# Layer 0 of a two-layer attention trunk: attention steps ordered by a planner, with half of the output projection placed among them

## The chip, the core and the metric

The kernel runs on one core of one Trainium2 chip. The metric is the device time of one execution in microseconds; the kernel before was timed at 2638.1 us (median of three runs, 2637.88 to 2638.44).

## What is computed

A decoder trunk on 1024 positions of width 1024, in float32, two layers. Layer 0 mixes with sparse attention of three branches, layer 1 with forgetting attention; both add four heads of attention into 256 memory tokens, project all heads with one output matrix, add the residual, and end with a gated feed-forward block. Only layer 0's attention and its output projection are touched:

```python
def block(args):                        # layer 0, 12 heads in 2 groups
    s = einsum(qc, kc) * scale          # 64 compressed blocks
    p_cmp = masked_softmax(s, cmp_end[None, :] <= t[:, None])
    ...                                 # with 16 blocks of 64 and top 16: all causal keys
    s = einsum(qc, kg) * scale
    p = masked_softmax(s, m_sel)
    ...                                 # keys of the last 512 positions
    s = einsum(qc, kw) * scale
    p = masked_softmax(s, m_win)
    return g[..., 0:1] * o_cmp + g[..., 1:2] * o_slc + g[..., 2:3] * o_win
...
o_mem = memory_attention(q_mem, mem, mem_norm[l], w_mem_kv[l])
x = x + concatenate([o_mix, o_mem], axis=-1) @ w_o[l]
x = x + conv_ffn(rms_norm(x, ffn_norm[l]), w_up[l], conv_w[l], conv_b[l], w_down[l])
```

## The kernel before

Every float32 operand of a matmul is split into an upper part (rounded to the matmul's input type, written by ScalarE, line 81) and a lower part (the rest, written by VectorE, line 82); `mm3` (lines 156 to 158) makes one product from three matmuls of up to 512 columns.

The work of layer 0 follows in this order: `layer0_proj` (norm, keys, values, compressed keys, the queries of heads 0 to 3), `layer0_attn` (attention), `out_proj` (output projection, residual, norm), then the feed-forward block.

Attention is cut into units: one head and one half `c` of the queries (`c` = 0 is the first 512 positions). There are 24 units of the three-branch attention and 8 units of memory attention. For a unit, the scores of a row tile go to a two-bank PSUM tile `psa` (line 301, two such tiles exist); VectorE takes the row maximum (line 318), ScalarE the exponent with its sum into SBUF (lines 334 and 337); VectorE inverts the sum (lines 346 and 347) and GpSimd scales by that and the gate (line 358). Then TensorE transposes 128x128 pieces into PSUM `psb` (line 391; four such banks), four to a step; ScalarE writes their upper part `pt` (line 398), VectorE the lower part (line 401), and TensorE multiplies both with the values (line 414) into the unit's output in another `psb`. A finished unit is copied to `ob` (line 504) and stored to DRAM (line 506); when both heads of a pair of rows are there, `operand` loads them again (line 471), adds the two halves on GpSimd (line 472) and splits them into `oT`.

The exponents of each of the four kinds (selected or window branch, `c` 0 or 1) have a buffer of their own (tags `ps0`, `ps1`, `pw0`, `pw1`, one each; memory units `pm`, two). The order is written by `attention`: at every step `k` it emits the maxima and exponents of the scores begun one step ago, the transposes of step `k`, new scores as `pace` has due, one slice of the projection of later queries while such work lasts (`work`, `rope_proj`, `plain_proj`), and the value products of step `k - 2`. Tile's scheduler then fixes each engine's order.

The units run head by head, `c` = 0 and 1 in turn. `out_proj` comes behind the last unit: for each half `n` of the columns and each of 8 row tiles, 24 matmuls of 512 columns into a `psb` bank, an addition to the residual `x` (line 862), and in the second half the norm of the finished row tile (`norm_part`), its transposes (line 894) and splits. All DMAs are issued by SyncE in one queue, in order.

## Time and profile before

| what | value |
| --- | --- |
| median of three runs | 2638.1 us |
| profiled execution, its own time | 2643.0 us |
| its span | 2640.9 us |
| TensorE busy | 2506.7 us, 95% |
| VectorE, ScalarE, GpSimd busy | 71%, 50%, 28% |
| layer 0's attention, first score to last value product | 192 to 673 us |
| layer 0's output projection | 672 to 765 us |

How to read it: the span is what the profiler saw between the first and last instruction. Matmuls overlap in the pipeline, so the duration of one (some 0.39 us at 512 columns) is longer than the distance from its start to the next one's start when nothing is waited for, and TensorE can count as busy while it is slowed by a late operand. For TensorE the count of matmuls in a stretch, times that distance, tells more than its busy share.

### The profile page before, as it was taken

To read this page: it belongs to the slowest core of one execution; us is meant where nothing else is said; L and a number is where in the kernel's file an instruction comes from. 1 tells how busy PE (TensorE), PEld (TensorE's weight loads), DVE (VectorE), ACT (ScalarE), POOL (GpSimd) and SP (SyncE) were. 2 spreads that over 40 slices of the span, in tenths; PEclk is the share of its full clock that TensorE was granted. 3 is DMA by queue.
4 is the path that set the end of the run, shared out by engine and by line. 5 is a ranking of instruction groups with operands and counts; after the bars stand their busy time and mean duration, and the time that the engine had idled before them with its cause. 6 is when DMAs were issued, how large, how long until landed. Compare 5 with 4: busy or idle time off the path is not lost.

```text
span 2640.9 us, 36023 instructions
## 1 busy us (share of the span) xinstructions
PE 2506.7 (95%) x12642; PEld 2073.0 (78%) x12642; DVE 1881.6 (71%) x2822; ACT 1331.5 (50%) x2553; POOL 751.2 (28%) x616
## 2 busy tenths in 40 slices
PE   7899899988999999998999999999999999998998
PEld 6787777776877888886888988887777888886886
DVE  5757677878377787877765467778576877787765
ACT  4437576768245454544454356656334545443443
POOL 0105344445133545543000000000223555454000
PEclk9999999999999999999999999999999999999999
DMA  8473123334422323337434556656532333337523
GB/s 243 142 206 109 53 81 100 89 108 136 153 88 82 102 96 109 108 125 273 133 128 128 160 171 194 188 177 181 197 112 69 104 112 100 101 105 262 186 90 118
DMA packets 302702, 357.72 MB, mean 135 GB/s; under 512 B 37961, under 2 KB 183225, under 8 KB 302521
## 3 DMA queue, kind: packets, MB, share of 16 engines
q1 hardware_dynamic: 302520, 355.41, 42.8%
q8 instruction: 100, 1.64, 0.3%
q14 instruction: 82, 0.66, 0.1%
HBM read 245.55 MB, written 109.78 MB: 135 GB/s over the span
## 4 chain that ended last, share of the span: by engine, by line
PE 71%; DVE 9%; DMA 6%; ACT 6%; POOL 4%; issue 3%; SPq 1%; POOLq 0%; ACTq 0%; DVEq 0%
PE psa L156 11%; PE psa L157 11%; PE psa L158 11%; PE psb L156 8%; PE psb L158 8%; PE psb L157 8%; PE psa L301 5%; PE psb L414 4%; PE psb L391 3%; DVE pt L401 2%; DVE stat L318 2%; POOL gs L1350 1%; DMA hT<-in_w_down_dram 1%; ACT ps L334 1%; POOL pw L358 1%
## 5 line engine op out<-in xcount | busy, mean ns | idle before, releaser
L81 ACT ACTIVATE wh<-wr 128x512 fp32r<-128x512 f32 (+2 forms) x254 | 193.1, 765 | 353.9 <-PE psb L158 147.2
L82 DVE TENSOR_TENSOR wl<-wr,wh 128x512 fp32r<-128x512 f32 (+2 forms) x254 | 241.6, 955 | 165.5 <-ACT wh L81 164.8
L1335 DVE SCALAR_TENSOR_TENSOR v<-u,cw,v 128x1023 f32<-128x1023 f32 (+1 forms) x176 | 273.1, 1552 | 68.7 <-ACT v L1333 65.8
L401 DVE TENSOR_TENSOR pt<-psb,pt 128x512 fp32r<-128x512 f32 (+2 forms) x380 | 245.7, 657 | 87.2 <-ACT pt L398 84.6
L398 ACT ACTIVATE pt<-psb 128x512 fp32r<-128x512 f32 (+2 forms) x380 | 217.5, 583 | 130.9 <-PE psb L391 129.5
L1333 ACT ACTIVATE v<-u,cw 128x1024 f32<-128x1024 f32 x88 | 109.6, 1245 | 310.2 <-DVE u L1322 283.4
L414 PE MATMUL psb<-pt,vv 128*128 128x512 f32 (+2 forms) x864 | 232.2, 366 | 12.4 <-DVE pt L401 9.0
L156 PE MATMUL psa<-hT,wh 128*128 128x512 f32 x560 | 219.2, 392 | 5.3 <-DVE u L1296 5.3
L301 PE MATMUL psa<-kk,qq 128*128 128x512 f32 (+4 forms) x792 | 196.4, 359 | 25.0 <-ACT ps L334 14.7
L158 PE MATMUL psa<-hT,wl 128*128 128x512 f32 x560 | 218.6, 390 | 0.8 <-DVE wl L82 0.8
L157 PE MATMUL psa<-hT,wh 128*128 128x512 f32 x560 | 218.5, 390 | 0.0
L318 DVE TENSOR_REDUCE stat<-psa 128x1 f32<-128x640 f32 (+7 forms) x288 | 200.6, 714 | 21.5 <-PE psa L301 20.3
L334 ACT ACTIVATE ps<-psa,stat 128x128 f32<-128x128 f32 (+2 forms) x224 | 156.7, 706 | 59.6 <-DVE stat L318 53.7
L120 POOL TENSOR_TENSOR rs<-ss,consts 128x1 f32<-128x1 f32 x44 | 25.8, 588 | 516.3 <-DVE ss L118 378.0
L472 POOL TENSOR_TENSOR wr<-wr 128x512 f32<-128x512 f32 x32 | 42.3, 1323 | 440.7 <-DMA wr<-o 426.6
L414 PEld LDWEIGHTS psb<-pt,vv 128*128 128x128 f32 x864 | 141.4, 195 | 30.8 <-DVE pt L401 16.1
L301 PEld LDWEIGHTS psa<-kk,qq 128*128 128x128 f32 x792 | 125.8, 194 | 47.3 <-ACT ps L334 23.6
L156 PE MATMUL psb<-hT,wh 128*128 128x512 f32 x384 | 160.0, 417 | 2.2 <-DVE rt L607 1.8
L156 PE MATMUL psb<-wh 128*128 128x512 f32 x352 | 139.3, 396 | 20.7 <-ACT wh L81 20.6
L1237 POOL TENSOR_TENSOR ws<-wr 128x512 f32<-128x512 f32 x44 | 74.7, 1699 | 295.6 <-DMA wr<-in_w_up_dram 213.2
L391 PE MATMUL psb<-consts,ps 128*128 128x128 f32 x928 | 150.7, 280 | 8.1 <-DVE pt L401 4.9
L158 PE MATMUL psb<-hT,wl 128*128 128x512 f32 x384 | 151.7, 395 | 0.0
(285 smaller groups left out, 6853.1 us busy)
## 6 DMA issues: line engine op xcount, KB each, us to landing
wr<-in_w_up_dram SPq DMA_DIRECT2D x88, 512.0 KB
wr<-gd SPq DMA_DIRECT2D x154, 256.0 KB
gd<-v SPq DMA_DIRECT2D x88, 256.0 KB
gd<-gs SPq DMA_DIRECT2D x66, 256.0 KB
o<-ob SPq DMA_DIRECT2D x128, 128.0 KB
wr<-o SPq DMA_DIRECT2D x32, 512.0 KB
hT<-in_w_down_dram SPq DMA_DIRECT2D x64, 256.0 KB
qd<-st SPq DMA_DIRECT2D x56, 256.0 KB
```

Of the source, the lines that this page charges most:

```text
L81: nc.scalar.activation(hi, src, AF.Copy)
L82: nc.vector.tensor_tensor(lo, src, f32(hi), ALU.subtract)
L156: mm(out, lh, rh, start=first, stop=False, skip_group_check=more)
L157: mm(out, lh, rl, start=False, stop=False, skip_group_check=more)
L158: mm(out, ll, rh, start=False, stop=last, skip_group_check=more)
L301: nc.tensor.matmul(out, w, rhs, start=b not in banks[:i], stop=b not in banks[i + 1:])
L318: nc.vector.reduce_max(br["stat"][:, 0, ii:ii + 1], s[:, o:o + w], axis=AX.X, negate=True)
L391: nc.tensor.transpose(tp[0:kb, x:x + P], br["pt"][ii][:, o:o + kb], self.ident)
L398: nc.scalar.activation(st["hi"], st["src"], AF.Copy)
L401: self.nc.vector.tensor_tensor(st["lo"], st["src"], f32(st["hi"]), ALU.subtract)
L414: self.nc.tensor.matmul(out, v, t, start=st["begin"] and i == 0, stop=st["end"] and i == len(mms) - 1)
L1335: nc.vector.scalar_tensor_tensor(v[:, d:], u[:, :S - d], cw[:, tap, i:i + 1], v[:, d:], ALU.mult, ALU.add)
```

## The change

A class `Plan` is added. Every piece of layer 0's attention stage becomes a task with an engine, a duration written into the code, the tasks that it waits for, a priority and the buffers that it takes and gives back. `Plan.run` plays the tasks through such engines, each engine starting the ready task with the lowest priority number, and the tasks are then emitted in the order of their starts; Tile keeps that order on TensorE, ScalarE, VectorE and GpSimd (`manual_schedule`). SyncE's DMAs are still ordered by Tile.

Besides the order: the two value products of a step (from the upper and from the lower part) are tasks of their own. The four exponent tags and `pm` become one tag `p` of three buffers. The units are reordered: heads 0 to 5 as before with the first-half memory units among them, then for heads 6 to 11 the `c` = 0 units run ahead of the `c` = 1 units (`a` and `b` in the code). The output projection of the first 512 positions (`out_tasks`, 8 tiles of 24 matmuls) is cut into pieces of 6 matmuls that stand among the attention steps; its result with the residual goes to DRAM (`xr`). `out_half` then does the other 512 positions; it loads `w_o`'s first column half a second time, and normalises row tiles 0 to 3, read back from `xr`, in its first half. The lower parts of weights and rotated queries and keys are written by GpSimd in place of VectorE; the factor `QSC` moves into the rotation's tables; the gates are laid out so that the copy and product per unit (lines 826 and 828) fall away.

```diff
+    def run(self):
...
+            for e in engines:
+                skipped, q = [], ready[e]
+                while q and not busy[e]:
+                    x = heapq.heappop(q)
+                    t = self.tasks[x[1]]
+                    if not self.can(t):
+                        skipped.append(x)
+                        continue
+                    self.take(t["acq"], 1)
+                    order.append(t)
...
+                    heapq.heappush(events, (now + t["us"], 1, t["id"]))
...
+            t["fn"]()
+
...
-    def split(self, src, hi, lo, scale=None):
+    def split(self, src, hi, lo, scale=None, low=None):
...
             nc.scalar.activation(hi, src, AF.Copy)
-            nc.vector.tensor_tensor(lo, src, f32(hi), ALU.subtract)
...
+    def planned(self, ap, pool, l, od, units, works, lead, src):
...
+        steps, users, done, last = [], {}, {}, ([], [])
...
+        start = pl.add("SP", 15.0, lambda: None)
...
+                tag, _, bufs = br["p"]
+                same = users.setdefault(tag, [])
+                br["before"] = same[-bufs] if len(same) >= bufs else None
+                same.append(br)
+            deps = [(done[n, u["at"][1]], 6.0) for n in u["needs"]] + [start]
+            deps += [s_last[k - 2] if k > 1 else None, w_last[k - 3] if k > 2 else None, *(n_last[k - 4] if k > 3 else ())]
+            deps += [x for i in u.get("takes", ()) for x in (s_last[i], w_last[i])]
...
+                           [t_prev] + [ready[id(x[0]), ii] for x in st["ps"] for ii in x[2]], q, ["tp"])
+                hi = pl.add("ACT", 0.18 + 0.82e-3 * n, lambda st=st: self.upper_p(ap, st), [t], q, ["pt"])
+                lo = pl.add("DVE", 0.15 + 1.04e-3 * n, lambda st=st: self.lower_p(st), [hi], q, (), ["tp"])
+                us, o = sum(self.columns(len(x[2]) * P) for x in st["ps"]), ["o"] if st["begin"] else ()
+                if st["ps"][0][0]["kb"] == P:
+                    v = pl.add("PE", us, lambda st=st: self.value(st, 0), [hi, v_prev], q + 1.5, o)
+                    v_prev = pl.add("PE", us, lambda st=st: self.value(st, 1), [lo, v], q + 1.6, (), ["pt"])
+                else:
+                    v_prev = pl.add("PE", us, lambda st=st: self.value(st, 0), [lo, v_prev], q + 1.6, o, ["pt"])
...
+        k0, k1 = max(k for (c, _), ts in outs.items() if c == 0 for _, k in ts) + 6, len(steps) + 2
+        xr, w_o = self.dp.tile([CH, D], F32, name=f"xr{l}"), {}
+        before = [None, None]
+        for n in range(2):
+            prio = [k0 + (k1 - k0) * (16 * n + i) / 32 for i in range(16)]
+            ws = [self.w_o_tasks(pl, l, w_o, k, n, [split, before[-1]], prio[0] - 4) for k in range(0, KT, 2)]
+            for t in range(4):
+                before.append(self.out_tasks(pl, pool, oT[0], w_o, n, t, ws, [parts[0, kt] for kt in range(KT)], before[-2:], prio[4 * t:4 * t + 4],
+                                             src, xr))
...
+    def out_tasks(self, pl, pool, o, w_o, n, t, ws, parts, before, prio, src, xr):
...
+        def mms(i):
+            if i == 0:
+                x["ps"] = self.psb()
+            for k in range(2):
+                kt = 2 * i + k
+                wh, wl = w_o[n, i]
+                self.mm3(x["ps"], [p[:, kt, t * P:(t + 1) * P] for p in o["t"]], (wh[:, k, :], wl[:, k, :]), kt == 0, kt == KT - 1)
+
+        def add():
+            nc.vector.tensor_tensor(x["x"], x["ps"], x["x"], ALU.add)
+            nc.sync.dma_start(xr[t * P:(t + 1) * P, cs], x["x"])
+        ld, pe = pl.add("SP", 0.0, load, [ws[0], before[0]], prio[0]), before[1]
+        for i in range(4):
+            pe = pl.add("PE", 1.37, lambda i=i: mms(i), [pe, ws[i], parts[2 * i], parts[2 * i + 1]], prio[i], ["pb"] if i == 0 else (),
+                        ["wh"] if t == 3 else ())
+            pl.fill.append(pe)
+        return pl.add("DVE", 0.7, add, [pe, (ld, 4.0)], prio[3], (), ["pb"])
...
+                        def lo(half=half, s_=s_):
+                            st = x["st", half]
+                            nc.gpsimd.tensor_tensor(st[:, 1, :], x["r", half], f32(st[:, 0, :]), ALU.subtract)
...
         w = self.a["a_w_in"][0]
         self.n_pt, self.n_q = 3, 2
         with self.tc.tile_pool(name="l0a", bufs=1) as ap:
-            def mem_q(m):
...
+            def mem_q(m, *at):
+                return self.plain_tasks(("m", m), at, cpool, h, w, 1572 + m * P, self.qm0, m, QSC)
+            works = [self.rope_tasks(("q", 1), ((-3, 30), (30, 58)), cpool, h, w, 256, self.qd0, P), mem_q(0, (58, 68), (140, 150)), mem_q(1, (68, 80), (150, 160)),
+                     self.rope_tasks(("q", 2), ((80, 115), (118, 140)), cpool, h, w, 512, self.qd0, 2 * P)]
...
-            mem = list(self.mem_units(ap, self.qm0, self.mem[0], [("pm", 1024, 2)] * 2, lambda h: ("m", h // 2), "pool"))
-            units = nsa[:12] + mem[0:2] + nsa[12:16] + mem[2:4] + nsa[16:20] + mem[4:6] + nsa[20:22] + mem[6:8] + nsa[22:]
-            return self.attention(ap, 0, od, units, work, 6, 9)
...
+
+            a, b, c, d = nsa[12::2], nsa[13::2], mem[0::2], mem[1::2]
+            units = nsa[:8] + c[0:1] + nsa[8:10] + c[1:2] + nsa[10:12] + c[2:4]
+            g1 = len(units)
+            units += a[0:2] + b[0:1] + a[2:4] + b[1:2] + a[4:6] + b[2:3] + d[0:1] + b[3:4] + d[1:2] + b[4:5] + d[2:4] + b[5:6]
...
+            self.n_ob = 1
+            return self.planned(ap, cpool, 0, od, units, works, 5, self.a["x"][0])
...
-        t_s, t_w, t_c = [("ps0", 1280, 1), ("ps1", 3328, 1)], [("pw0", 1280, 1), ("pw1", 2560, 1)], ("pc", 256, 2)
+        t_s, t_w, t_c = [("p", 3328, 3)] * 2, [("p", 3328, 3)] * 2, ("pc", 256, 2)
...
-                        gt = self.sb(ap, [P, 3, 4], F32, "gt", 2)
-                        nc.vector.tensor_copy(gt, self.gates[:, c * 4:(c + 1) * 4, h * 3:(h + 1) * 3].rearrange("p t b -> p b t"))
-                        if c == 0:
-                            nc.vector.tensor_tensor(gt[:, 0, 0:1], gt[:, 0, 0:1], self.rv, ALU.mult)
+                        gt = self.gates[:, c, h * 3:(h + 1) * 3, :]
...
+    def out_half(self, l, oT, pool, fx, up, src):
...
+        self.residual(pool, src, xr, (0, 4, 1, 5, 2, 6, 3, 7))
+        for n in (1, 0):
+            if n == 0:
+                w = self.load_block(a["w_o"][l], [(0, CH)])
+                up.load(0)
...
+                ps, o = two[:, t % 2 * CH:(t % 2 + 1) * CH], (t - 4) * P
+                for i, kt in enumerate((0, 1, 2, 6, 7, 3, 4, 5)):
+                    self.mm3(ps, (oT[1][0][:, kt, o:o + P], oT[1][1][:, kt, o:o + P]), w(kt, 0, CH), i == 0, i == KT - 1)
+                xs = self.x[:, t, n * CH:(n + 1) * CH]
+                nc.vector.tensor_tensor(xs, ps, xs, ALU.add)
...
+                for f in turns:
+                    f()
...
-    def residual(self, pool, src):
+    def residual(self, pool, src, first, order):
         self.x = pool.tile([P, NT, D], F32, name=self.nm("x"))
-        for t in range(NT):
-            self.nc.sync.dma_start(self.x[:, t, :], src[t * P:(t + 1) * P, :])
+        for t in order:
```

TensorE at the head of the attention stage. The first rows are of the kernel before: `psb_1913` is a projection tile of later queries (heads 4 to 7), `psa_1685` and `psa_1736` the first unit's scores.

```order
L157 MATMUL psb_1913<-hT_93,wh_1697 128x512
L158 MATMUL psb_1913<-hT_92,wl_1698 128x512
L301 MATMUL psa_1685<-kk_261_1657,qq_265_1672 128x128
L301 MATMUL psa_1736<-kk_261_1657,qq_265_1672 128x512
L301 MATMUL psa_1685<-kk_261_1657,qq_266_1673 128x128
```

The same place in the changed kernel: `psb_1710` and `psb_1798` are such projection tiles, `psa_1773` and `psa_1787` the first unit's scores.

```order
L246 MATMUL psb_1710<-hT_91,wh_1672 128x512
L247 MATMUL psb_1710<-hT_90,wl_1673 128x512
L390 MATMUL psa_1773<-kk_273_1729,qq_277_1744 128x128
L390 MATMUL psa_1773<-kk_273_1729,qq_278_1745 128x128
...
L390 MATMUL psa_1787<-kk_273_1729,qq_278_1745 128x512
L390 LDWEIGHTS identb
L390 MATMUL psa_1787<-caub,identb 128x128
L245 MATMUL psb_1798<-hT_92,wh_1669 128x512
L246 MATMUL psb_1798<-hT_93,wh_1669 128x512
```

Before, 96 projection matmuls of later queries (four tiles of 24) stand ahead of the first score; now 48 do, and the other 48 come behind it.

TensorE near the end of the attention stage. Before, in the last unit (`psb_7428` is its output), transposes and value products alone:

```order
L391 MATMUL psb_7451<-consts,ps_1189_7111 128x128 x4
L414 MATMUL psb_7428<-pt_7436,vv_4407 128x512 x2
L391 MATMUL psb_7466<-consts,pw_1211_7233 128x128 x4
L414 MATMUL psb_7428<-pt_7446,vv_4407 128x512 x2
L391 MATMUL psb_7476<-consts,ps_1189_7111 128x128 x2
```

Now, in the last unit (`psb_7617` is its output), with a tile of the output projection, `psb_7600`:

```order
L390 MATMUL psa_7584<-winb,identb 128x128
L390 LDWEIGHTS identb
L390 MATMUL psa_7584<-wcb,identb 128x192
L492 MATMUL psb_7593<-consts,p_7473 128x128 x4
L245 MATMUL psb_7600<-wh_7188,hT_4040 128x512
L246 MATMUL psb_7600<-wl_7189,hT_4040 128x512
L247 MATMUL psb_7600<-wh_7188,hT_4041 128x512
...
L492 MATMUL psb_7612<-consts,p_7473 128x128 x4
L516 MATMUL psb_7617<-pt_7607,vv_4701 128x512
```

Six projection matmuls now stand between two transposes of the last unit; all eight tiles of the first half stand ahead of the last value product.

SyncE's queue behind the attention stage. Before (`wr` are the three buffers for raw operands, `xm` the residual's copy in DRAM):

```order
L471 DMA wr_7554<-o_1_1653 128x2x512
...
L1091 DMA x_7577<-in_x_dram 128x1024 x8
L189 DMA wr_7800<-in_w_o_dram 128x2x512
L189 DMA wr_7806<-in_w_o_dram 128x2x512
L189 DMA wr_7812<-in_w_o_dram 128x2x512
L189 DMA wr_7818<-in_w_o_dram 128x2x512
L849 DMA wr_7824<-in_ffn_norm_dram 128x1024
```

Now:

```order
L797 DMA wr_7776<-o_1_1654 128x2x512
...
L1555 DMA x_7800<-in_x_dram 128x1024
L1364 DMA xm_75<-x_7800 128x1024 x4
L278 DMA wr_7994<-in_w_o_dram 128x2x512
L278 DMA wr_8000<-in_w_o_dram 128x2x512
L278 DMA wr_8006<-in_w_o_dram 128x2x512
L278 DMA wr_8012<-in_w_o_dram 128x2x512
L1695 DMA wr_8018<-in_w_up_dram 128x8x128
```

Four stores of `x` now stand ahead of the loads of `w_o`, and the norm's gain (`in_ffn_norm`), which stood behind them, was loaded earlier and holds one of the three `wr` buffers.

## Rows read from the trace of the kernel before

**Rows 1.** Page, part 1: busy time, share of the span and instructions of each engine.

```profile
PE 2506.7 (95%) x12642; PEld 2073.0 (78%) x12642; DVE 1881.6 (71%) x2822; ACT 1331.5 (50%) x2553; POOL 751.2 (28%) x616
```

**Rows 2.** Busy time of each engine in stretches (us of the span: length, busy us and count of PE, PEld, DVE, ACT, POOL, granted clock as a share of full, DMA share, GB/s). Four stretches of layer 0's attention, then one of layer 1's.

```profile
200.00:250.00 50.00, 45.20 (x282) 35.50 (x281) 41.30 (x91) 34.41 (x89) 26.72 (x36) 1.00 0.41 123
...
300.00:350.00 50.00, 45.02 (x279) 36.69 (x279) 34.01 (x78) 32.53 (x85) 19.87 (x29) 0.93 0.21 56
...
450.00:500.00 50.00, 47.64 (x320) 39.57 (x321) 39.87 (x88) 38.61 (x104) 25.32 (x31) 1.00 0.34 97
...
600.00:650.00 50.00, 41.65 (x262) 33.20 (x263) 42.25 (x82) 39.40 (x100) 27.25 (x32) 0.97 0.45 130
...
1600.00:1650.00 50.00, 49.38 (x283) 40.14 (x282) 42.42 (x95) 35.62 (x97) 0.00 (x0) 1.00 0.73 199
```

**Rows 3.** The same view for the whole attention stage of layer 0 and the projection behind it.

```profile
190.00:672.00 482.00, 433.02 (x2739) 351.68 (x2738) 369.56 (x758) 336.96 (x852) 215.76 (x271) 0.98 0.34 97
672.00:765.00 93.00, 89.80 (x411) 73.81 (x410) 37.88 (x51) 18.47 (x30) 12.29 (x12) 0.98 0.37 134
```

**Rows 4.** Groups of TensorE's matmuls by shape in 190 to 672 us: those of 512 columns (but one) and of 384 (busy us, mean ns, idle before).

```profile
L301 PE MATMUL psa<-kk,qq 128*128 128x512 f32 x240 | 97.6, 457 | 22.9 <-ACT ps L334 12.9 <-ACT pc L337 8.9 <-DMA qq<-qd 0.5
L414 PE MATMUL psb<-pt,vv 128*128 128x512 f32 x216 | 79.2, 439 | 7.3 <-DVE pt L401 5.5 <-ACT pt L398 1.6
...
L414 PE MATMUL psb<-pt,vv 128*128 128x384 f32 x120 | 43.8, 410 | 1.9 <-DVE pt L401 1.4 <-ACT pt L398 0.5
L156 PE MATMUL psb<-hT,wh 128*128 128x512 f32 x67 | 28.2, 421 | 1.8 <-DVE rt L607 1.8
...
L158 PE MATMUL psb<-hT,wl 128*128 128x512 f32 x68 | 27.1, 398 | 0.0
L157 PE MATMUL psb<-hT,wh 128*128 128x512 f32 x68 | 26.9, 396 | 0.0
L301 PE MATMUL psa<-kk,qq 128*128 128x384 f32 x72 | 24.5, 380 | 0.0
...
L414 PE MATMUL psb<-pt,mv 128*128 128x512 f32 x32 | 11.9, 443 | 0.6 <-DVE pt L401 0.6
L414 PE MATMUL psb<-pt,vc 128*128 128x512 f32 x23 | 11.4, 495 | 3.4 <-DVE pt L401 3.4
```

**Rows 5.** Timeline of TensorE (start, duration): a step of the last unit of layer 0, and two matmuls of the output projection, 48 starts apart.

```profile
662.17 0.60 PE L391 MATMUL psb<-consts,ps 128*128 128x128 f32 x4
...
663.07 0.60 PE L391 MATMUL psb<-consts,ps 128*128 128x128 f32 x4
...
680.05 0.39 PE L156 MATMUL psb<-wh,hT 128*128 128x512 f32 x1
...
690.93 0.39 PE L156 MATMUL psb<-wh,hT 128*128 128x512 f32 x1
```

**Rows 6.** Waits in 190 to 680 us, who waited for whom (total us, times, longest).

```profile
DVE gt L826 <- POOL stat L352: 19.6, 13, 2.2
PEld psa L301 <- ACT ps L334: 19.1, 22, 2.7
...
PEld psb L414 <- DVE pt L401: 17.4, 25, 2.6
```

**Rows 7.** Timeline of TensorE and of SyncE's queue at the head of the attention stage.

```profile
191.91 0.39 PE L158 MATMUL psb<-hT,wl 128*128 128x512 f32 x1
192.14 0.56 PE L301 MATMUL psa<-kk,qq 128*128 128x128 f32 x3
...
183.04 6.71 SPq L824 DMA_DIRECT2D qq<-qd  x8
```

**Rows 8.** Groups of VectorE and of GpSimd in 190 to 672 us.

```profile
L82 DVE TENSOR_TENSOR wl<-wr,wh 128x1024 fp32r<-128x1024 f32 x5 | 7.1, 1422 | 4.6 <-ACT wh L81 4.6
L85 DVE SCALAR_TENSOR_TENSOR st<-rt,st 128x512 fp32r<-128x512 f32 x8 | 5.7, 729 | 0.0
L828 DVE TENSOR_TENSOR gt<-gt,consts 128x1 f32<-128x1 f32 x11 | 5.3, 481 | 0.2
L826 DVE COPY gt<-gates 128x12 f32<-128x12 f32 x22 | 3.8, 170 | 19.7 <-POOL stat L352 19.6
...
L613 POOL TENSOR_TENSOR rt<-rt,rt 128x512 f32<-128x512 f32 x8 | 10.7, 1342 | 28.6 <-DVE rt L612 27.7 <-ACT st L84 0.9
```

**Rows 9.** Timeline behind the last value product of the attention (which ends at 672.66 us): the loads of `x` in SyncE's queue, and the lower part of the projection's last operand on VectorE.

```profile
679.08 4.41 SPq L1091 DMA_DIRECT2D x<-in_x_dram  x8
...
682.46 0.69 DVE L82 TENSOR_TENSOR hT<-wr,hT 128x512 fp32r<-128x512 f32 x1 [9.86 <-ACT hT L81]
```

**Rows 10.** Timeline of TensorE around its one long stop in the output projection.

```profile
736.71 1.88 PE L894 MATMUL psb<-consts,x 128*128 128x128 f32 x8 [2.72 <-DVE x L902]
...
738.82 0.63 PE L157 MATMUL psb<-wl,hT 128*128 128x512 f32 x1
```

**Rows 11.** Two VectorE lines over the whole span (count, duration min/median/max in ns, first and last start): line 401 reads PSUM and SBUF, line 902 reads two SBUF tensors.

```profile
L401 DVE TENSOR_TENSOR pt<-psb,pt x380: 398/682/694, 216.5 to 1869.1; 128x512 fp32r<-128x512 f32 x160, 128x256 fp32r<-128x256 f32 x18, 64x512 fp32r<-64x512 f32 x12
...
L902 DVE SCALAR_TENSOR_TENSOR x<-x,rs,wr x16: 1272/1285/2314, 729.7 to 1977.9; 128x1024 f32<-128x1024 f32 x16
```

**Rows 12.** Timeline of a late unit's way from its scores to its scaled exponents, on TensorE and on GpSimd.

```profile
640.80 1.08 PE L301 MATMUL psa<-kk,qq 128*128 128x512 f32 x4 [1.19 <-ACT ps L334]
...
647.77 5.05 POOL L358 TENSOR_SCALAR ps<-ps,stat,gt 128x640 f32<-128x640 f32 x4 [3.60 <-DVE stat L320]
```

433 lines of the change are left out of this document (377 added, 56 removed).

## The prediction

> **What bounds the kernel now.** I began with the page's busy times: TensorE 95%, the next engine 71% [rows 1]. That looks like a kernel with nothing left to gain, and the next view corrects it. In the table of stretches one counts matmuls and not busy time. A stretch of layer 1's attention has 283 matmuls in 50 us, 88 of them of a projection at 512 columns, and TensorE at 49.4 us [rows 2]; layer 0's attention has about as many in a stretch, but hardly any at full width.
>
> So I price the pure matmul time of layer 0's attention. Matmuls of 512 columns start 0.227 us apart when nothing is waited for (48 starts in 10.88 us); a step of four transposes and two such products repeats after 0.90 us, which leaves 0.111 us for one transpose [rows 5]. In 190 to 672 us there are 2739 matmuls [rows 3], 715 of them of 512 columns (one more than the rows' sum of 714), 192 of 384 [rows 4], and 1832 smaller ones. I price 384 columns in proportion, 0.17 us, the smaller ones as a transpose: 162.3 + 32.6 + 203.4 = 398.3 us. Nine of the wide ones (2.0 us) come before the first score at 192.1 us [rows 7]. That leaves **396.3 us of work in the 479.9 us** from there to 672.0 us: a rate of 0.826, and 84 us in which TensorE is slowed or stands. A mean matmul of the stage costs 0.1455 us; by that 300 to 350 us runs at 0.81, 450 to 500 us (memory units in it) at 0.93, 600 to 650 us at 0.76 [rows 2].
>
> What ends the waits: mostly scores that wait until ScalarE has read one of the two `psa`, then value products that wait for the lower part [rows 4, 6]. No engine is full: VectorE is at 369.6 of 482 us, ScalarE 337.0, GpSimd 215.8 [rows 3]. The stage is bound by the order in which four engines hand work to each other, and by the lack of other TensorE work to put into the gaps. The projection behind it is bound by TensorE: 384 matmuls, 87.2 us, at 89.8 busy of 93 us [rows 3].
>
> **The change, part by part.**
>
> *Work of TensorE.* It computes the same products. To the stage come 192 matmuls of the output projection's first half, 43.6 us, and 48 of a query projection that stood ahead of the first score, 10.9 us. The stage then holds 396.3 + 43.6 + 10.9 = 450.8 us of work, and 43.6 us stay behind it.
>
> *The head of the stage.* The 96 projection matmuls ahead of the first score cover the load of keys, values and queries: SyncE issues the last query load at about 189.7 us, and the first score starts right behind the last of them at 192.1 us [rows 7]. With 48, TensorE gets to the first score at 181.2 us and stands, since the scores are ahead of the other projection in its queue. The loads themselves are the same ones in the same order, so I let the first score start at 191.5 us (bounds: 181.2, if the loads were not what it waited for, and 194). After its one long stop of 2.7 us, TensorE's matmuls took 0.63 us instead of 0.39 [rows 5, 10]; ten idle us should slow the next few us likewise, 2 us (0 to 4). So this edit gains nothing by itself: it moves 10.9 us of filler to where gaps are, and pays about as much for it.
>
> *The rate.* This carries the forecast. I cut the stage by its order on TensorE. **A**, 248 us of work up to the middle heads, holds ten projection tiles, 54 us or 22%. **B**, 97 us, has almost none. **C**, the last 106 us, has 180 of the 192 projection matmuls, 41 us or 38%. For C the nearest row is layer 1's stretch, where projection makes 88 x 0.227 = 20.0 us: with the other 195 matmuls at 0.138 us (layer 0's mean without its projection, 351 us over 2536) it runs at 0.94, by its busy time at 0.99; I take 0.96. For B the bounds are 0.81 (300 to 350 us, few projection matmuls) and 0.93 (450 to 500 us); I take 0.88, in the middle, because the order now sets a score where its `psa` is due back, and each value product of an upper part no longer stands in one piece with that of the lower part. For A, between 0.82 (200 to 250 us by the same count) and 0.96, I take 0.92: more filler than B, less than C. So 248 / 0.92 + 97 / 0.88 + 106 / 0.96 = 269.6 + 110.2 + 110.4 = **490 us**. With all the lower ends (0.82, 0.81, 0.94) it is 535 us, with all the upper ones (0.96, 0.93, 0.99) 470 us.
>
> *VectorE, ScalarE, GpSimd.* From VectorE go 33 gate operations (9.1 us) and with them 19.6 us in which it stood in its queue for GpSimd; the lower parts of weights and rotated queries (12.8 us) [rows 6, 8]; eight additions of 0.69 us come. About 353 us remain, 72% of 490. GpSimd gets 16 operations like line 613's 1.34 us and ten of double width (1.9 to 2.7 us): 215.8 + 21 + 23 = 260 us, 53%. ScalarE has four weight tiles more, near 342 us, 70%. None becomes the bound at a rate of 0.92; all this is inside the rate.
>
> GpSimd's operation beside it is what stretches a VectorE operation on two SBUF tensors here: line 902 takes 1.28 us, and 2.31 us at most; line 401, which reads PSUM, never passes 0.694 us [rows 11]. The Trainium skill (GPSIMD Engine Reference, Specifications) says that GpSimd shares its SBUF interfaces with VectorE and contends with two-input instructions, and (Key points) that VectorE is about twice as fast at elementwise work, both of which speak against moving lower parts. By it the 16 remaining two-input lower parts of the stage would be stretched, some 16 x 0.6 = 9 us of VectorE's spare time, by the rows of line 902 no more than 16 us: the sum stays.
>
> *Behind the stage.* The last unit's way to the projection took from 672.7 to 683.2 us, 10.5 us [rows 9]. Half the projection no longer covers it; TensorE's order has 38 projection matmuls (8.6 us) ahead of that operand, so it stands some 2 us. Next, the second loads of `w_o` wait in SyncE's queue behind four stores of `x`, and these for loads of `x` that were issued from 6.4 to 10.8 us behind the last product; with two free `wr` buffers the four weight tiles come in pairs. TensorE needs the first after 21.8 us. I count 3 us more than the old projection's own stops (bounds 0 and 10).
>
> *Sum*, against the profiled execution (span 2640.9 us, its own time 2643.0; the median of the runs is 2638.1, so I apply the difference to that). Before: the stage ends at 672.0 us, with 87.2 us behind: 759.2. After: 191.5 + 2 + 490.2 = 683.7, with 43.6 + 3 behind: 730.3. The difference is -28.9 us: **2609 us**.
>
> **Rivals.** *Slower: the fixed order stalls.* From its scores to the first scaled tile a late branch took 7 to 8 us (640.8 to 648.8 us) [rows 12]. By the order before, some 15 to 22 us of matmul work lie between a branch's first scores and its first transpose; now 8 to 19 us, since three `p` buffers serve where four and two did. TensorE takes its queue in order, so each delay that the code's durations leave out stops it, with the projection pieces queued behind. The Trainium skill (TensorE: Matmul & The Clock Gate, Architectural detail) has ScalarE and VectorE as strict queues and lets only weight loads be pulled ahead on TensorE; no row here shows otherwise. It decides where the rate falls under 450.8 / 519.1 = 0.868. At the old 0.826 the stage takes 545.8 us: 193.5 + 545.8 + 46.6 = 785.9, 2665 us. For it: the small leads. Against: VectorE loses its 19.6 us of waits for GpSimd, and 0.826 was reached with a tail at 0.76 that now holds filler.
>
> *The filler alone works.* The order brings nothing in A and B (0.86 for its share of filler, 0.82), C gets 0.96: 288.4 + 118.3 + 110.4 = 517.1 us, which only repays the head: 2636 us.
>
> *As good as layer 1.* The stage runs at 0.96 throughout: 469.6 us, 2589 us. For it: layer 1's stretch has VectorE at 42.4 us of 50 and loses nothing. Against: it has twice the filler.
>
> **How the numbers follow.** About 0.2%, 5 us, is what a measurement of this kernel can tell from no change. The forecast stands for rates of 0.89 to 0.945 and has a chance of 0.50; as good as layer 1 0.20; the filler alone 0.14; slower 0.16. Faster by over 5 us takes the first two and 0.04 of the third: 0.74. Within it lie 0.09 and slower 0.17. The range, 2585 to 2648 us, takes in the upper ends of the rates below, and above the case of filler alone with 10 us of stops behind the stage; the rest of the slower case is left out.
>
> **What would show it.** Right: an idle stretch of some 10 us on TensorE ahead of the first score, ended by the query loads; the last value product of the attention at 675 to 695 us; stretches at the stage's end at 49 us busy or more; waits of scores for ScalarE at half of the former; no gate operation on VectorE. A stop before the second weight half, ended by VectorE's lower part of `w_o`, would show the term behind the stage. Wrong: the last value product behind 715 us, with long waits of transposes for GpSimd.

## The result, and the profile after

The changed kernel takes 2653.9 us in the median of five runs (2647.7 to 2656.1), against 2638.4 us: a ratio of 1.0054, 95% interval 1.0043 to 1.0066. Measured again on another occasion (`c0_after`), ten runs gave 1.0032 (1.0020 to 1.0045). It is slower by 0.3 to 0.5%, some 8 to 15 us, where I forecast 29 us faster.

The profiled execution has a span of 2652.1 us, 11.2 us more than before. Three moments cut this difference into parts. First the timeline of TensorE in the kernel after: the first score, the last value product, and the first product of the feed-forward block that reads `vh` (start, duration, idle time before it and what ended it).

```profile
193.59 0.78 PE L390 MATMUL psa<-kk,qq 128*128 128x128 f32 x2 [11.24 <-DMA qq<-qd]
...
702.53 0.50 PE L516 MATMUL psb<-pt,vc 128*128 128x512 f32 x1
...
815.51 0.50 PE L245 MATMUL psa<-hT,vh 128*128 128x512 f32 x1
```

The last two of these in the kernel before, in the same view:

```profile
672.66 0.50 PE L414 MATMUL psb<-pt,vc 128*128 128x512 f32 x1
...
810.78 0.51 PE L156 MATMUL psa<-hT,vh 128*128 128x512 f32 x1
```

The attention ends at 703.03 us in place of 673.16 (in [rows 9] I gave 672.66 us as its end, which is the start of that product): +29.9 us, where I had forecast +11.7. From there to the common product it takes 112.5 us in place of 137.6: -25.1 us, where I had forecast -40.6. So at 815 us the kernel is 4.7 us behind. The other 6.5 us of the profile arise in code that the change leaves alone. The same two moments in the profile of `c0_after`:

```profile
705.72 0.50 PE L516 MATMUL psb<-pt,vc 128*128 128x512 f32 x1
...
818.34 0.50 PE L245 MATMUL psa<-hT,vh 128*128 128x512 f32 x1
```

There the product is 7.6 us late and the span (2648.7 us) 7.8 us longer: nothing is added later. From this product to the end the kernel before takes 1830.1 us, the profiled execution of the changed kernel 1836.6, and the profiles of all other runs below 1827 to 1833. So those 6.5 us belong to that one execution; what made them is open. The two profiles also show how far single profiles of one kernel differ: their attention ends 3.2 us apart.

The stretches of the attention again (columns as in [rows 2]), its three parts A, B and C (ends at about 469 and 581 us, where TensorE had done 248 and 345 us of work), and the projection behind it:

```profile
200.00:250.00 50.00, 48.87 (x319) 40.83 (x317) 38.06 (x80) 36.23 (x91) 26.44 (x36) 1.00 0.35 101
300.00:350.00 50.00, 47.95 (x314) 40.93 (x313) 38.14 (x81) 35.10 (x93) 20.61 (x30) 0.97 0.30 83
437.00:473.00 36.00, 29.80 (x168) 23.58 (x167) 21.53 (x48) 25.36 (x67) 26.38 (x28) 0.95 0.69 213
...
600.00:650.00 50.00, 43.13 (x227) 35.54 (x226) 26.66 (x48) 26.84 (x62) 22.35 (x19) 0.86 0.36 107
...
193.50:469.00 275.50, 260.73 (x1632) 217.07 (x1632) 199.30 (x405) 193.58 (x491) 145.87 (x170) 0.98 0.42 120
469.00:581.00 112.00, 104.56 (x710) 86.53 (x708) 93.91 (x195) 87.23 (x225) 58.12 (x81) 1.00 0.34 91
581.00:703.00 122.00, 113.33 (x636) 93.79 (x635) 68.84 (x119) 64.91 (x144) 44.16 (x40) 0.94 0.30 91
...
703.00:765.00 62.00, 51.34 (x211) 38.63 (x209) 25.96 (x39) 18.79 (x30) 12.29 (x12) 0.89 0.54 192
```

The first two rows are what the order was meant to bring: 319 and 314 matmuls in 50 us where there were 282 and 279 [rows 2]. The next two are where it is lost: 168 in 36 us, which would be 233 in 50, and a tail with a granted clock of 0.86. The last row answers the projection of [rows 3]: busy 83% where it was 97%.

What [rows 6] showed has shrunk. TensorE's waits in 193 to 680 us now, who waited for whom:

```profile
PEld psa L390 <- ACT pc L426: 6.5, 5, 2.9
PEld psa L390 <- ACT p L423: 4.4, 7, 1.0
...
PEld psb L516 <- DVE pt L506: 2.1, 5, 0.7
```

They were 19.1 us for the exponent of a full branch and 17.4 for the lower part; no gate operation is left on VectorE. The waits that the change aimed at are mostly gone. Other losses have come, in three places.

**GpSimd in the middle.** Its timeline in the poor stretch:

```profile
438.43 2.38 POOL L822 TENSOR_TENSOR wl<-wr,wh 128x1024 fp32r<-128x1024 f32 x1 [8.63 <-ACT wh L819]
441.22 2.38 POOL L460 TENSOR_SCALAR p<-p,stat,gates 128x128 f32<-128x128 f32 x4 [0.41 <-DVE stat L435]
446.33 4.69 POOL L822 TENSOR_TENSOR wl<-wr,wh 128x1024 fp32r<-128x1024 f32 x2 [2.73 <-ACT wh L819]
451.60 2.38 POOL L460 TENSOR_SCALAR p<-p,stat,gates 128x128 f32<-128x128 f32 x4 [0.57 <-ACT pt L503]
...
456.52 2.39 POOL L822 TENSOR_TENSOR wl<-wr,wh 128x1024 fp32r<-128x1024 f32 x1
```

The four `wl` are lower parts of `w_o`. Their first product stands at 469 us, the bulk behind 580 us. The planner starts any task that is ready as soon as its engine is free, whatever its due time, so 9.5 us of GpSimd, and the upper parts on ScalarE, stand among the scaling of exponents, and while GpSimd waits for an upper part (8.63 us) it scales nothing. That this delays the scaling is not shown by these rows: the one at 441.22 us had to wait 0.41 us more for VectorE.

**TensorE in the tail.** Its stops behind 600 us:

```profile
604.35 0.87 PE L390 MATMUL psa<-kk,qq 128*128 128x512 f32 x4 [2.26 <-DMA qq<-qd]
...
639.51 0.35 PE L390 MATMUL psa<-mk,qq 128*128 128x256 f32 x1 [2.48 <-DMA qq<-qm]
640.34 1.83 PE L390 MATMUL psa<-mk,qq 128*128 128x256 f32 x7 [0.48 <-DMA qq<-qm]
644.25 1.09 PE L492 MATMUL psb<-consts,p 128*128 128x128 f32 x4 [1.65 <-DVE pt L506]
```

Two stops wait for query loads. The planner counts 4.0 us from the start of a unit's loads to its scores; the first load of the unit that starts at 604.35 us is issued at 597.7, 6.6 us ahead. SyncE's queue is held up in this tail by the projection itself. What its DMAs waited for in 600.79 to 703 us (total us, times, longest):

```profile
SPq L843 <- DVE rt L842: 31.3, 5, 10.9
```

These are stores of the half projection (`xr`) that stand in the queue until VectorE has added the residual, and query loads stand behind them.

**TensorE behind the attention,** where the projection before ran nearly without a break:

```profile
713.87 0.50 PE L245 MATMUL psa<-wh,hT 128*128 128x512 f32 x1 [2.23 <-ACT hT L802]
...
726.18 0.50 PE L245 MATMUL psa<-wh,hT 128*128 128x512 f32 x1 [1.38 <-DVE ss L207]
...
734.97 1.06 PE L1358 MATMUL psb<-consts,x 128*128 128x128 f32 x8 [1.28 <-DVE x L1366]
...
737.72 0.73 PE L245 MATMUL psa<-wh,hT 128*128 128x512 f32 x2 [1.34 <-ACT wh L170]
...
741.10 0.63 PE L247 MATMUL psa<-wh,hT 128*128 128x512 f32 x1
...
746.76 0.73 PE L245 MATMUL psa<-wh,hT 128*128 128x512 f32 x2 [1.52 <-ACT wh L170]
```

And SyncE's queue there:

```profile
714.54 8.02 SPq L1364 DMA_DIRECT2D xm<-x  x4
722.61 19.38 SPq L278 DMA_DIRECT2D wr<-in_w_o_dram  x4
```

In turn TensorE waits for the last operand, for norms of row tiles 0 to 3 on VectorE (twice), and twice for a tile of `w_o` whose load stood behind the four stores of `x`. Behind a stop, matmuls come 0.43 us apart for a while (0.63 us each, as in [rows 10]); the granted clock is then at its lower level, 1.2 GHz:

```profile
739.00:742.00 3.00, 2.67 (x10) 1.92 (x9) 3.00 (x6) 1.19 (x2) 0.00 (x0) 0.50 0.16 26
```

### The profile page after: what moved, and what is told of

The parts are those of the page before. It is cut to its first block, busy times and chain, and to the rows that moved or that the text cites. A ratio compares the mean times of both kernels' runs of the same rounds, so it can differ in the third digit from the quotient of the medians.

```text
span 2652.1 us, 36075 instructions
## 1 busy us (share of the span) xinstructions
PE 2511.5 (95%) x12642; PEld 2081.2 (78%) x12642; DVE 1850.8 (70%) x2749; ACT 1337.6 (50%) x2557; POOL 817.7 (31%) x658
## 4 chain that ended last, share of the span: by engine, by line
PE 72%; DVE 7%; DMA 7%; ACT 4%; POOL 3%; issue 2%; SPq 1%; POOLq 0%; ACTq 0%; DVEq 0%
PE psa L245 11%; PE psa L246 11%; PE psa L247 11%; PE psb L245 8%; PE psb L247 8%; PE psb L246 8%; PE psa L390 6%; PE psb L492 4%; PE psb L516 4%; POOL gs L1815 1%; DVE pt L506 1%; DMA hT<-in_w_down_dram 1%; DVE stat L407 1%; DVE wl L171 1%; ACT pt L503 1%
## 5 line engine op out<-in xcount | busy, mean ns | idle before, releaser
L170 ACT ACTIVATE wh<-wr 128x512 fp32r<-128x512 f32 (+2 forms) x240 | 181.8, 761 | 312.4 <-PE psb L247 115.6
L171 DVE TENSOR_TENSOR wl<-wr,wh 128x512 fp32r<-128x512 f32 (+2 forms) x232 | 222.9, 962 | 148.4 <-ACT wh L170 148.0
L516 PE MATMUL psb<-pt,vv 128*128 128x512 f32 (+2 forms) x864 | 252.7, 370 | 4.9 <-DVE pt L506 2.5
L390 PE MATMUL psa<-kk,qq 128*128 128x512 f32 (+4 forms) x792 | 186.7, 347 | 23.4 <-DMA qq<-qd 13.9
L460 POOL TENSOR_SCALAR p<-p,stat,gates 128x128 f32<-128x128 f32 (+1 forms) x192 | 149.8, 795 | 183.0 <-DVE stat L435 126.2
L423 ACT ACTIVATE p<-psa,stat 128x128 f32<-128x128 f32 (+2 forms) x224 | 149.1, 672 | 49.6 <-DVE stat L409 19.4
L576 POOL TENSOR_TENSOR wr<-wr 128x512 f32<-128x512 f32 x16 | 21.0, 1312 | 424.9 <-DMA wr<-o 423.4
```

The lines of the kernel that those rows point to most:

```text
L170: nc.scalar.activation(hi, src, AF.Copy)
L171: (low or nc.vector).tensor_tensor(lo, src, f32(hi), ALU.subtract)
L390: nc.tensor.matmul(out, w, rhs, start=b not in banks[:i], stop=b not in banks[i + 1:])
L460: eng.tensor_scalar(br["pt"][ii], br["pt"][ii], r[:, ii:ii + 1], br["gate"][:, ii:ii + 1], ALU.mult, ALU.mult)
L516: self.nc.tensor.matmul(u["o"][:, iis[0] * P:iis[0] * P + w], br["v"](j), t[:, x:x + w], start=st["begin"] and first and i == 0, stop=st[" ...
```

## The experiments

The numbers are ratios to the kernel before, run beside it on the same chip, with 95% intervals.

**The changed kernel again** (`c0_after`), no edit.

> The changed kernel itself, on the same chip and beside the same runs of before as the next kernels, since single runs of one kernel differ by some us. If the 1.0054 is the kernel's own: 1.0045 to 1.0065 again, 2650 to 2656 us. In its first profile layer 1's untouched output projection was 5.4 us slower than in the kernel before, in the profiles of the first four experiments it was not: if that was chance, it is gone here and the ratio is nearer 1.002 to 1.004.

1.0032 (1.0020 to 1.0045). The slowdown is the kernel's own. Its size was 1.0054 the first time, and what made that difference is open.

**The order alone** (`e5_nofill`): the planned order, the whole projection behind it in `out_proj`, as before. The rest of the change (shared buffers, lower parts on GpSimd, the layout of the gates) stays in.

```diff
-        for n in range(2):
-            prio = [k0 + (k1 - k0) * (16 * n + i) / 32 for i in range(16)]
...
-                before.append(self.out_tasks(pl, pool, oT[0], w_o, n, t, ws, [parts[0, kt] for kt in range(KT)], before[-2:], prio[4 * t:4 * t + 4],
-                                             src, xr))
+        for k in range(0, KT, 2):
+            self.w_o_tasks(pl, l, w_o, k, 0, [split], len(steps) - 12)
...
-        return [oT[c]["t"] for c in range(2)], at, xr, gain["t"]
+        return [oT[c]["t"] for c in range(2)], at
```

> The planned order of the attention alone: the whole output projection stands behind it, as in the kernel before. The stage then holds 407 us of work. If the order is good by itself (a rate of 0.87, as in the middle part of the stage in the changed kernel): it ends at 662 us, with the old projection's 87.2 us behind it some 10 us earlier than before, 2628 us. If the order brings nothing (0.826): it ends at 687 us, 2654 us. If the pieces of projection are what slows it (0.93 without them): 631 us, 2597 us. It also shows whether layer 1's second out projection is slower by 6 us without any change to it.

0.9998 (0.9988 to 1.0008): no difference from the kernel before, and 0.3% faster than the changed kernel. This run is the most telling one, as both kernels place the attention alike up to step 200 of 250. There the transposes of that step, without and with projection, on TensorE's timeline of `e5_nofill`:

```profile
599.96 1.06 PE L492 MATMUL psb<-consts,p 128*128 128x128 f32 x4
...
669.18 0.50 PE L516 MATMUL psb<-pt,vc 128*128 128x512 f32 x1
...
808.46 0.50 PE L245 MATMUL psa<-hT,vh 128*128 128x512 f32 x1
```

and of the changed kernel, in its first profile and in `c0_after`:

```profile
600.79 0.60 PE L492 MATMUL psb<-consts,p 128*128 128x128 f32 x4
```

```profile
604.98 0.60 PE L492 MATMUL psb<-consts,p 128*128 128x128 f32 x4
```

Up to there the changed kernel has done 48 projection matmuls more (by lines, 16 of each of the three, 10.9 us of work) and has lost 0.8 us in the one profile and 5.0 us in the other: half of their work or more was hidden. From there to the end of the attention, `e5_nofill` takes 69.7 us and the changed kernel 102.2 us (101.2 in `c0_after`). The difference is 32.5 us, and the other 144 projection matmuls are 32.7 us of work. Together they cost their full price, though TensorE has idle time in that tail without them. By stretches of just this tail, of `e5_nofill`:

```profile
599.96:669.68 69.72, 59.15 (x364) 47.40 (x363) 49.18 (x84) 46.16 (x105) 26.69 (x26) 0.97 0.23 67
```

and of the changed kernel:

```profile
600.79:703.03 102.24, 93.57 (x515) 77.17 (x514) 56.69 (x97) 52.85 (x117) 40.06 (x36) 0.93 0.30 89
```

TensorE stands for 10.6 us without the projection and for 8.7 us with it, and the mean granted clock is 0.93 in place of 0.97 (0.95 in `c0_after`).

**Late weights** (`e6_late`: the changed kernel; `e7_nofill_late`: the order alone). A `w_o` tile is loaded and split only when a given step's transposes have begun.

```diff
-            ws = [self.w_o_tasks(pl, l, w_o, k, n, [split, before[-1]], prio[0] - 4) for k in range(0, KT, 2)]
+            ws = [self.w_o_tasks(pl, l, w_o, k, n, [split, before[-1], None if n else steps[140 + 6 * k]["turn"]], prio[0] - 4) for k in range(0, KT, 2)]
...
-            self.w_o_tasks(pl, l, w_o, k, 0, [split], len(steps) - 12)
+            self.w_o_tasks(pl, l, w_o, k, 0, [split, steps[200 + 6 * k]["turn"]], len(steps) - 12)
```

> Against the changed kernel in the same call. The four tiles of the output weight's second half-projection are not loaded and split as soon as the engines have a moment (428 to 460 us), but one by one later, tied to steps 140, 152, 164 and 176. Theory 'the planner starts such work greedily, far ahead of its use, and GpSimd's four splits of 2.4 us and ScalarE's stand before the scaling of exponents': the stretch 437 to 473 us gains up to 8 us, the kernel 4 to 8. Rival 'that stretch is slow from the loads of keys, values and queries and from the change of units': within 2 us, or the loss turns up at the new places.

1.0017 (1.0002 to 1.0032), beside 1.0032.

> Against the kernel with the planned order alone and the whole projection behind it (2637.6 us, 0.9998 of before). Its four weight tiles are tied to steps 200, 212, 224 and 236 in place of as soon as possible. By the same theory 4 to 8 us less: 2630 to 2634 us, faster than the kernel before by some 0.2%. Rival: within 2 us, 2636 to 2640.

0.9972 (0.9961 to 0.9983), beside 0.9998 for the order with early weights. The poor stretch, first of `e5_nofill`, then of `e7_nofill_late`:

```profile
437.00:473.00 36.00, 29.43 (x157) 23.14 (x156) 20.85 (x47) 24.82 (x66) 25.31 (x28) 0.91 0.64 194
```

```profile
437.00:473.00 36.00, 32.24 (x191) 26.97 (x191) 27.11 (x56) 23.57 (x63) 16.48 (x25) 0.91 0.50 152
```

191 matmuls in place of 157, and GpSimd at 16.5 us in place of 25.3. The last value product starts 6.6 us earlier than in `e5_nofill`, and all of that is gained ahead of step 200. Without projection the theory of work started too early holds. For the changed kernel it is not settled: the intervals of 1.0017 and 1.0032 overlap. In the profile of `e6_late`

```profile
698.55 0.50 PE L516 MATMUL psb<-pt,vc 128*128 128x512 f32 x1
...
814.45 0.50 PE L245 MATMUL psa<-hT,vh 128*128 128x512 f32 x1
```

the attention ends 4.0 us earlier than in the changed kernel's first profile, but 115.4 us follow up to the product with `vh` in place of 112.5, and 1.1 us is left. Nor is it shown what the early weights hold up: their loads, the upper parts on ScalarE and the lower parts on GpSimd were moved together. What this pair settles is the half projection: with late weights in both it is 1.0017 with it and 0.9972 without it, intervals apart.

**Lower parts back on VectorE** (`e8_dve`).

```diff
-        return pl.add("POOL", 1.95, lambda: nc.gpsimd.tensor_tensor(w_o[n, k0 // 2][1], ...
+        return pl.add("DVE", 1.25, lambda: nc.vector.tensor_tensor(w_o[n, k0 // 2][1], ...
```

(likewise for the weights and the rotated queries)

> Against the changed kernel in the same call. The lower parts of weights and rotated queries go back to VectorE, as in the kernel before, with VectorE's times told to the planner. If GpSimd's slower and queued lower parts stop the attention (POOL waited 20 us for ScalarE's upper parts with the scaling behind it): 3 to 8 us less. If VectorE is the fuller engine and the price is paid there: 3 to 8 us more, as the planner's own end is 8 us later than the changed kernel's. Theory that neither matters much: within 2 us.

1.0032 (1.0021 to 1.0042): no difference. Which of the two engines writes them does not matter here.

**Two output buffers** (`e3_ob2`).

```diff
-            self.n_ob = 1
+            self.n_ob = 2
```

> Against the changed kernel's 2653.9 us. Two output buffers in place of one, the order of all engines but SyncE as it was. ScalarE waited 12.5 us in four pieces for the store of the output before (6.0 us the longest, in the stretch 437 to 473 us in which some 8 us are lost). Theory 'a resource that the planner leaves out stops the fixed order': 4 to 8 us less, 2646 to 2650. Rival 'these waits were beside the path, the stretch is lost to loads and GpSimd': within 2 us.

1.0028 (1.0017 to 1.0039). ScalarE's waits for the store are gone from its profile, and the kernel is as slow as the changed one (1.0032). The rival holds: those waits lay beside the path.

**Weights ahead of the stores** (`e4_wo`). `raw` loads two row blocks of `w_o`'s first column half; the other two loads stay where they were.

```diff
         self.residual(pool, src, xr, (0, 4, 1, 5, 2, 6, 3, 7))
+        for k0 in (0, 2):
+            raw(k0)
         for n in (1, 0):
```

> Against the changed kernel's 2653.9 us. Two of the four loads of the output weight's first column half go ahead of the four stores of x in SyncE's queue. Behind the attention TensorE is 18.9 us slower than in the kernel before. Theory 'the weights come late there': the stops of 1.3 and 1.5 us on ScalarE's upper parts at 737.7 and 746.8 us go, with the slowed matmuls behind them 5 to 8 us, 2646 to 2649. Rival 'they wait for a free buffer and for ScalarE and VectorE anyway, which are held up by the norms of row tiles 0 to 3': within 2 us.

1.0023 (1.0010 to 1.0036). In the profile

```profile
705.53 0.50 PE L516 MATMUL psb<-pt,vc 128*128 128x512 f32 x1
...
812.57 0.50 PE L245 MATMUL psa<-hT,vh 128*128 128x512 f32 x1
```

there are 106.5 us from the end of the attention (706.03 us) to the first product with `vh`, in place of 112.5: the 6 us expected, in that part. Of the other profiles that keep this part as it was, four (`c0_after`, `e1_head`, `e3_ob2`, `e8_dve`) have 112.1 to 112.3 us, and `e9_all` with this repair has 106.1. The ratio, 2 to 3 us better than 1.0032, shows less, and its interval overlaps.

**The head.** First the planner's start (`e1_head` on the changed kernel, `e10_best` on the order alone with late weights):

```diff
-        start = pl.add("SP", 15.0, lambda: None)
+        start = pl.add("SP", 26.0, lambda: None)
```

> Against the changed kernel's 2653.9 us. The planner is told that the keys, values and queries land 26 instead of 15 us after its start, so it puts 72 projection matmuls instead of 48 ahead of the first score (5.4 of the 11.2 us in which TensorE stood there). If the head's idle time is an independent loss: 5 us less, 2649. If the stage pays for filler as much as it gains (my forecast's 'this edit gains nothing by itself'): within 2 us. If the order is sensitive to any change of its numbers: a shift of either sign by up to 10 us.

> The planned order alone with late weights (0.9972 of before, 2633 us), and the planner told that the first loads land 26 instead of 15 us after its start, so that 72 instead of 48 projection matmuls stand ahead of the first score. If the head's idle time is a loss of its own: up to 5 us less, 0.995. If the filler is only moved: within 2 us. The planner's own end, counted from the first score, is 2.1 us sooner.

1.0013 (1.0004 to 1.0022), beside 1.0032, and 0.9984 (0.9974 to 0.9993), beside 0.9972. Neither tests what I meant, and why the first came out some 5 us better than the changed kernel (the intervals just overlap) is open. On TensorE's timeline of `e10_best` the first score comes 7 us later than without the edit (in `e1_head` likewise, at 200.79 us):

```profile
200.95 0.72 PE L390 MATMUL psa<-kk,qq 128*128 128x128 f32 x2 [14.75 <-DMA qq<-qd]
```

The number also sets where the loads stand in SyncE's queue, and they moved back behind stores and tables. So a second try told only the first unit's scores to come later (`e13_head`):

```diff
-                    s = pl.add("PE", s_us, lambda it=it: self.score(it), [s_prev, (ld, 4.0)], prio, ["psa"])
+                    s = pl.add("PE", s_us, lambda it=it: self.score(it), [s_prev, (ld, 4.0 if k else 15.0)], prio, ["psa"])
```

> The planned order without filler and with late weights (0.9972), and only the first unit's scores are told to come 15 instead of 4 us behind their loads; SyncE's queue up to these loads stays as it was. In the earlier try with the planner's start at 26 us the loads themselves moved back (first score at 201 us in place of 194), so it said nothing of the idle head. 72 instead of 48 projection matmuls now stand ahead of the first score, which should stay at 194 us. My forecast's step 'this moves filler to where gaps are and pays as much for it': within 2 us of 0.9972. Rival 'the idle 11 us are a loss of their own': up to 5.4 us less, 0.995.

0.9989 (0.9980 to 0.9998). Now TensorE stands half as long, at the same first score:

```profile
192.90 0.91 PE L390 MATMUL psa<-kk,qq 128*128 128x128 f32 x2 [6.00 <-DMA qq<-qd]
```

and the kernel is not faster than 0.9972. The step "gains nothing by itself" holds in this kernel: from the first score to the end of the attention it takes 472.8 us in place of 469.0 (`e7_nofill_late`), though 5.4 us of projection have left that stretch.

**The old order of units** (`e11_units`), planned, late weights, no projection in the stage.

```diff
-            units += a[0:2] + b[0:1] + a[2:4] + ...
+            units = nsa[:12] + mem[0:2] + nsa[12:16] + mem[2:4] + nsa[16:20] + mem[4:6] + nsa[20:22] + mem[6:8] + nsa[22:]
```

> The planned order alone with late weights (0.9972), but the units in the order of the kernel before (both halves of a head in turn, memory units at their old places, memory queries projected earlier to suit). If the list scheduler is what gained and the order of units is neutral: 0.997 again. If three shared exponent buffers need the new order of units: some 10 us slower (the planner's own end is 13.2 us later), 1.000 to 1.002.

1.0023 (1.0014 to 1.0032), beside 0.9972: with three shared exponent buffers the old order costs 13 us, and the planner with it is slower than the kernel before. Its memory queries are also projected earlier, so the order of units is not quite alone in this.

**All three repairs** (`e9_all`: `e1_head`, `e4_wo` and `e6_late` in one).

> The changed kernel with three repairs at once: 24 more projection matmuls ahead of the first score (1.0013 alone), the first weight tiles of the output projection tied to steps 140 to 176 (1.0017 alone), two of the second loads of the weight ahead of the stores of x (1.0023 alone, 5.9 us in its profile behind the stage). The changed kernel beside them: 1.0032. If their gains add: 4 + 4 + 4 us less than 1.0032, some 0.9985, 2636 us; if the half projection in the stage is a net loss even so, it stays above the kernel without it and with late weights (0.9972). If the repaired version passes that one, my reading that the filler itself does not pay is wrong.

1.0006 (0.9995 to 1.0017): no difference from the kernel before, and not as good as the order without projection in the stage.

**A quarter of the projection** (`e12_quarter`): only 96 matmuls, one column half of the first 512 positions, stand in the stage, with late weights. Behind it stands `out_proj` in place of `out_half`: no norm in its first half, and its loads of `w_o` ahead of the stores of `x`.

```diff
-        for n in range(2):
+        for n in range(1):
...
-            for t in range(NT):
+            for t in range(0 if n else done, NT):
```

(`done` is 4 in layer 0)

> Only one column half of the first 512 positions' projection (96 matmuls, 21.8 us) stands among the attention steps, with late weights; the other 288 matmuls stand behind the stage, the weight is loaded there once more as in the kernel before. To be compared with the same order without any filler (0.9972 of before) and with the whole first half in the stage and late weights (1.0017). Theory 'the tail of the stage has room for some 10 us of projection, and the way of the last unit, the loads of x and the norms need some 65 us of cover': the stage pays 12 us for 21.8, behind it the loss is under 4 us; 6 to 8 us less than without filler, 0.994 to 0.995. Rival 'any projection piece in the stage costs what it saves, and half a cover already loses': 0.997 to 0.999. Rival 'the loss behind the stage is in proportion to the cover that is gone': 8 us of it, 0.997.

0.9962 (0.9949 to 0.9975), 2629.8 us: faster than the kernel before and than the changed one, and by 0.001 than `e7_nofill_late`, which is not clear of noise. TensorE's timeline in its profile:

```profile
674.59 0.50 PE L516 MATMUL psb<-pt,vc 128*128 128x512 f32 x1
...
794.37 0.50 PE L245 MATMUL psa<-hT,vh 128*128 128x512 f32 x1
```

The same two in `e7_nofill_late`:

```profile
662.54 0.50 PE L516 MATMUL psb<-pt,vc 128*128 128x512 f32 x1
...
799.89 0.50 PE L245 MATMUL psa<-hT,vh 128*128 128x512 f32 x1
```

The stage pays 12.1 us for 21.8 us of projection. Of the 96 matmuls 60 (13.6 us of work) stand behind step 200. The tail from that step on, of `e7_nofill_late`:

```profile
592.80:663.04 70.24, 59.95 (x364) 46.59 (x363) 50.07 (x86) 49.88 (x109) 36.65 (x31) 0.98 0.29 85
```

and of `e12_quarter`:

```profile
597.61:675.09 77.48, 69.89 (x427) 56.61 (x426) 53.73 (x90) 48.24 (x113) 29.48 (x31) 1.00 0.26 77
```

It is 7.2 us longer (7.1 in `e15_qh` against `e13_head`), with a granted clock of 1.00, so the tail does take in part of its filler when there is less of it. With all 144 and late weights (`e6_late`) it takes 101.0 us: the further 84 matmuls, 19.1 us of work, cost 23.6. In this tail of `e12_quarter` SyncE waits 1.7 us for VectorE's sums, where it waited 31 us in the changed kernel, `c0_after` and `e6_late`, and no stop of TensorE there ends with a query load. That this queue is the cause is not shown by a run of its own.

Behind the stage there are 119.3 us in place of 136.9, 17.6 less: of the 21.8 us moved away 4.2 come back as loss (6.1 in `e15_qh` against `e13_head`). With twice as much moved, `e5_nofill` against the changed kernel, it is 138.8 against 112.5: 26.3 of 43.6, a loss of 17.3. So the loss is not in proportion to what was moved. How much of the further 11 to 13 us comes from missing cover, and how much from `out_half` with its early norms and its order of loads, these runs do not separate.

**Both** (`e15_qh`: `e12_quarter` with the edit of `e13_head`).

> Both: one column half in the stage with late weights, and 72 projection matmuls ahead of the first score. If the two effects add: the sum of the two differences from 0.9972, at best 0.992 (2619 us).

0.9958 (0.9943 to 0.9973): the same as `e12_quarter`.

## Why the prediction was wrong

**The head: right.** I forecast the first score at 191.5 us behind some 10 us of standing, with 2 us of slow matmuls; it came at 193.59 us behind 11.24. That the edit there only moves filler was shown by `e13_head`, for the order without projection.

**The rate in A and B: near.** A took 276 us (0.90, forecast 270 and 0.92); in the profile of `e6_late` it ends 5 us sooner, so the weights split early can make up that difference. B took 112 us (0.87, forecast 110 and 0.88). The waits of scores and value products are far smaller with the projection and without it (`e7_nofill_late`: 7.2 us for the exponent of a full branch, 5.9 for the lower part), so it is not the filler that removed them. Without its projection and with late weights, the change gains 0.3% (`e7_nofill_late`); the order, the shared buffers and the layout of the gates were not tried apart, save for the order of units, and without its new one the gain is gone (`e11_units`).

**The rate in C: the first wrong step.** "C, the last 106 us, [...] For C the nearest row is layer 1's stretch [...] I take 0.96." It took 122 us, 0.87. I took projection matmuls as filler that flows into whatever gap is there. The pair `e5_nofill` and changed kernel shows that the first 48 cost 0.8 to 5 us, half of their work or less, and that the other 144 together cost 32.5 us, all of their work; `e12_quarter` shows that 60 of them cost half of theirs. Up to step 200 there are eight pieces of 6; in the last 50 steps there are 24, one for every two steps, in a fixed order. A stretch with much projection in another stage said nothing of how this one would take it. What makes up the loss is only argued: query loads held up in SyncE's queue behind stores of the projection (the two stops on them are 2.3 and 3.0 us), a wait for VectorE, and slow matmuls behind them at a clock of 0.93. No run separates these.

**Behind the stage: the second wrong step.** "I count 3 us more than the old projection's own stops (bounds 0 and 10)." The term measured 18.5 us (112.5 us against the old 137.6 less the 43.6 moved away), 15.5 more than forecast and beyond my bound of 10. I priced the last operand (2 us, measured 2.2; its way before was 10.0 us and not 10.5, as the last value product ended at 673.16 us) and named the queue of `w_o` behind the stores, but took it as covered by 21.8 us of products; and I put the norms of row tiles 0 to 3, which now stand between the products, at nothing. The order of loads is some 6 us of it (`e4_wo`, in its profile). For the rest the cause stays open between missing cover and `out_half`'s norms: with 65 us of projection behind the stage in `out_proj` 4 to 6 us are lost, with 44 us in `out_half` 17.

**The rivals.** "The filler alone works" was wrong the other way round: the rest of the change gains a little, and half a projection as filler does not. In "slower: the fixed order stalls" the direction was right and the condition was not: the whole stage ran at 451 us of work in 509.4 us, 0.885, above the 0.868 that I had set as the turn, and the last value product came at 702.5 us, ahead of the 715 of my sign of being wrong. With 3 us behind it that would still have been a gain of some 11 us; the further 15.5 us behind it made it a loss.

**GpSimd.** That VectorE is about twice as fast at elementwise work, from the Trainium skill (GPSIMD Engine Reference, Key points), is nearly borne out for one operation: a lower part of 128x1024 takes 2.4 us on GpSimd, and took 1.4 us on VectorE [rows 8], a factor of 1.7. It did not decide, as `e8_dve` shows. VectorE's reads of PSUM were not stretched by GpSimd: line 506, the former 401 [rows 11], took at most 0.693 us. Line 902, with two SBUF operands, was: of its 16 operations in the kernel before, the four of 2.0 to 2.3 us ran beside operations of GpSimd, and the twelve of 1.3 us did not.

## What to carry to other kernels

Work that fills gaps on one engine may also have been cover for something else: price the stretch that it leaves with the same care as the one that it enters, and try half of the move first. Here a quarter of the projection cost nothing, and a half lost some 0.4% against none. A list scheduler that starts whatever is ready needs a "not before" beside its priority: in the order without projection this was worth 0.26%.

## What was not expected

144 projection matmuls placed in a tail with 10.6 of 69.7 us idle cost their full 32.7 us, while 60 of them cost about half of their work. The stores of their own result held SyncE's queue for 31 us there. And a number in the planner that should have moved work on TensorE only moved the first query loads by 7 us, because SyncE's queue follows the order in which tasks are emitted.
